# A two-layer hybrid transformer step on one core: low parts to VectorE, bank copies to ScalarE, layer 1's output projection by token groups, values woven into a norm

## The chip, the core and the metric

The kernel runs on one NeuronCore of a Trainium2 chip. Its engines are TensorE (PE: matmuls, which write PSUM banks), VectorE (DVE), ScalarE (ACT), GpSimd (POOL) and SyncE (SP, which issues most of the DMAs). Each engine works through its own queue in order. The metric is the device time of one execution in microseconds; the figure for a kernel is the median of its runs.

## The reference

One inference step for 1024 latent tokens and 128 context tokens, model width 1024, two layers with the same skeleton:

```python
hs = modulate(xs, norm_mix[i], sh1_s, sc1_s)      # RMSNorm, scaled and shifted by the condition
ms = mixer(hs)                                    # layer 0: pooling and latent attention; layer 1: neighbourhood attention
xs = xs + g1_s * ms                               # ms ends in an output projection, 1024 x 1024
xs = xs + g2_s * channel_mixer(modulate(xs, norm_mlp[i], sh2_s, sc2_s), mlp1[i], mlp2[i])
```

Layer 0 has 8 heads of latent attention with normed keys and queries (64 channels and 32 rotary ones); layer 1 has 16 heads whose queries and keys are normed, and each latent token attends to a window of 8 x 16 tokens and to all context tokens. `channel_mixer` is a squared-ReLU MLP of width 4096. Outputs are the two token sets and the new caches, all in float32.

## The kernel before, in words

Tokens lie along the free axis: every activation is a set of tiles of 128 channels by 1152 tokens (1024 latent, 128 context). Matmuls of full precision are made of three: each operand is split into a high part (rounded) and a low part (the rest), and `mm3` (L330 to L337) issues weight high by low, weight low by high, high by high. So a split is a cast (the high part) and a subtraction (the low part): `wsplit` (L156) for weights, `split_store` (L712 on) for key and query tiles of layer 0, `split_groups` (L908 on) and `split_acts` (L932 on) for the inputs of an output projection.

The program writes the work down in Python generators that `weave` (L130) interleaves by given lengths; a tile scheduler then settles the order on each engine from that text, from the dependencies, and from the buffers: PSUM has three pools of banks (`pa` 3, `pb` 3, `pc` 2), weights a ring of 3 raw and 4 + 4 split tiles, everything else 36 slots.

The stages, with the us at which they lie in the profile:

- to 200: modulation, layer 0's input projection and latents.
- 200 to 263, **key and query tiles**: `key_tile` (six tiles) and `query_tile` (six) multiply a tile by its norm factor, which a pair of `ps_b` matmuls (`bcast`, L707 and L708) spreads over the partitions, then `split_store` casts the tile (L715, ACT), subtracts (L716, the engine is an argument), and stores both parts to DRAM; `load_qk` and `load_rest` read them back by head. The keys' subtraction is on POOL, the queries' of tiles 4 and 0 on DVE, and that of tiles 1, 5, 2, 3 on POOL. `value_gen` (`ps_v`, L840 on) is woven with the maxima of the first head (`max_units`, L1073).
- 263 to 560: latent attention, head by head. `finish_values` (L1038 on) takes a finished PSUM bank: the numerators to the output tile (L1040, DVE), the sums to `den` (L1041, ACT); for every second head `recip_pair` (L1079 on) divides.
- 560 to 670 layer 0's output projection, by token groups (`out_group`), to 1430 its MLP. `first` (L446 to L448) and `second` (L476 to L478) are the MLP's two matmuls; `operand_gen` makes the former's operands (L352, ACT, and L353, DVE) from the normed input.
- 1430 to 1720, **layer 1's queries and keys** in four groups `g` (`ps_n1`), each followed by a norm: squares, `head_rstd`, 12 times a `bcast` and its product on DVE (L1266), and the split and store of four tiles (L1270, L1271). Then `value_gen1` (36 units; `ps_v`, L1427 to L1429) is woven with the maxima of heads 0 and 1 (`na_max`, L1320 and L1321).
- 1815 to 2125, **neighbourhood attention**: `na_units` computes scores (L1347, L1348), adds the bias table on DVE (L1373), takes the exponential on ACT (L1400) and multiplies by the values (L1380); `finish_values` as above. `na_max` of later heads runs between; its row of maxima goes through DRAM (`mrow`).
- 2090 to 2203, **layer 1's output projection** (`ps_o`, L335 to L337): `out_first` takes the first four input tiles (k = 0 to 3) for all tokens, 24 PSUM tiles of 384 columns, and adds them to the residual stream `x` (L342); it is woven into the last head and covers its end. `out_second` takes the other four, by chunks of 288 tokens, 32 PSUM tiles (L896); behind chunk 0 and chunk 1 stand the statistics of the MLP's norm (`norm_stats`, one `ps_n` matmul each, L274), and `operand_gen` runs between the tiles of chunks 2 and 3. The last pair of heads, which is finished last, is one of the four inputs of `out_second`.
- 2203 to the end: layer 1's MLP.

Of the kernel before, what the change touches and what calls it, by code (L numbers as in the profile page):

```python
# [32 lines left out]
XS, PSH, OW, OA, OB = (11, 11, 12, 12, 13, 13, 14, 14), (14, 14, 15, 15), 10, 8, 6  # L33
# [57 lines left out]
def hybrid_kernel(ctx: ExitStack, tc: tile.TileContext, I, O):  # L91
# [707 lines left out]
    def query_tile(t, eng):  # L799
        raw = tq[t]  # L800
        for ch in range(NCH):
# [15 lines left out]
          (chain(iter([None] * 7), *[key_tile(t, nc.gpsimd) for t in (4, 0, 1, 5, 2, 3)]), 38))  # L817
# [57 lines left out]

    def out_first(layer, acts):
        for q in range(4):
            ws = wout_chunk(layer, 0, q)
            for mi in range(2):
                for ch in range(NCH):  # L880
                    ps = PS("ps_o")[:, :CH]
                    mm3(ps, ws[mi], acts, ch * CH, ch * CH + CH)
                    residual(x, 2 * q + mi, ch, ps, layer, 0)
                    yield

    def out_second(layer, acts):
# [18 lines left out]
        free_acts(acts)  # L905
        return ops
# [24 lines left out]

    def split_acts(ops):  # L932
        acts = []
        for o in ops:
# [3 lines left out]
            nc.vector.tensor_sub(a[1], o, a[0])
# [99 lines left out]
    def finish_values(par, half, po, opair, den, last, store=None):  # L1038
        qs = slice(half * 512, half * 512 + 512)
        nc.vector.tensor_copy(opair[par:par + 64, qs], po[par:par + 64])  # L1040
        nc.scalar.copy(den[par:par + 64, qs], po[64 - par:128 - par])  # L1041
# [89 lines left out]
    for t in (1, 5, 2, 3):  # L1131
        run(query_tile(t, nc.gpsimd))
# [100 lines left out]
    r8 = S.alloc("r8h", F32R), S.alloc("r8l", F32R)  # L1233
    silu_load()
    for g in range(4):
# [16 lines left out]
        for ch in range(NCH):  # L1252
            cs = slice(ch * CH, ch * CH + CH)
            ps8 = PS("ps8", "pb")[0:8, :CH]
            for t in range(4):
                square_sum(ps8, t, raw[t][:, cs], t == 0, t == 3)
            head_rstd(ps8, 64, cs, nts[(NCH * g + ch) % 2], r8, rows)
        for ch in range(NCH):
            for t in range(4):
                wn = "naq" if t < 2 else "nak"  # L1260
                pp_ = pq if t < 2 else pk
                ps = PS("ps_b", "pb")[:, :CH]
                bcast(ps, t, r8, slice(ch * CH, ch * CH + CH), rows)
                for a, b, i in chunk_parts(ch):
                    o = pp_[:, pairs[t] * P:pairs[t] * P + P] if i else raw[t][:, a:b]
                    nc.vector.scalar_tensor_tensor(o, raw[t][:, a:b], V(wn), ps[:, a - ch * CH:b - ch * CH],  # L1266
                                                   op0=ALU.mult, op1=ALU.mult)
        for t in range(4):
            hi, lo = fhs[t % 2], raw[t].bitcast(F32R)
            nc.scalar.copy(hi[:, :NS], raw[t][:, :NS])  # L1270
            nc.vector.tensor_sub(lo[:, :NS], raw[t][:, :NS], hi[:, :NS])  # L1271
            dst, o = (qd, 0) if t < 2 else (kd, P)
            dma(dst[0][pairs[t], :, o:o + NS], hi[:, :NS])
            dma(dst[1][pairs[t], :, o:o + NS], lo[:, :NS])
# [133 lines left out]


    vt = []  # L1410

    def value_gen1():
        for qt in range(4):
            ws = [wsplit(I["wv1"][qt, i]) for i in range(2)]
            fs = slice(qt * 256, qt * 256 + 256)
            vt.append([S.alloc(f"vt{qt}{i}") for i in range(3)])
            v4 = [t.rearrange("p (a e f) -> p a e f", e=3, f=64) for t in vt[qt]]
            for t in v4:
                nc.gpsimd.memset(t[:, :, 1], 1.0)
            for i in range(2):  # L1420
                dma(v4[2][:, 4 + i, 0:3:2], I["v_cache"][:, qt * 256 + i * P:qt * 256 + i * P + P].rearrange("p (e f) -> p e f", f=64))
            for tt in range(9):
                ck = slice(tt * P, tt * P + P)
                ps = PS("ps_v1")[:, :256]
                for k in range(KD):
                    wh, wl = (w[:, (k % 4) * 256:(k % 4) * 256 + 256] for w in ws[k // 4])
                    nc.tensor.matmul(ps, hh[k][:, ck], wl, start=k == 0, stop=False)  # L1427
                    nc.tensor.matmul(ps, hl[k][:, ck], wh, start=False, stop=False)
                    nc.tensor.matmul(ps, hh[k][:, ck], wh, start=False, stop=k == KD - 1)  # L1429
                if tt == 8:  # L1430
                    nc.scalar.copy(pv[:, fs], ps)
                else:
                    nc.scalar.copy(v4[tt // 3][:, tt % 3 * 2:tt % 3 * 2 + 2, 0:3:2], ps.rearrange("p (g e f) -> p g e f", e=2, f=64))
                yield
# [222 lines left out]
```

## Time and profile before

| | us |
|---|---|
| three runs | 2985.49, 2983.98, 2985.34 |
| median | 2985.34 |
| profiled execution | 2996.6 |
| its span | 2994.7 |
| mean granted TensorE clock | 0.977 of full speed |

A row of the profile names the line of the program, the engine, the operation, the tiles it writes and reads, and their shape; then how many there are, their time together, the mean of one in ns, and the time for which the engine sat idle before them, with what ended it. A wait row has the waiting engine and line, what it waited for, the sum, how often, and the longest. A row of the timeline has the start, the length, and in brackets the idle time ahead of it. A row of the view by stretches has each engine's busy time in the stretch, the clock granted to TensorE, and the DMA engines' mean share. Idle time of an engine that is not the bottleneck costs nothing.

### The profile page before, as it was taken

The page shows a single profiled execution, that of the slowest core. Times are in us where ns is not written, and L with a number is a line of the kernel's source. Part 1 is how long each engine was busy: PE and PEld are TensorE (multiplying, and loading weights), DVE is VectorE, ACT ScalarE, POOL GpSimd, SP SyncE. Part 2 cuts the span into 40 slices and gives each one's busy share as a digit, 9 for nine tenths or more (in the row PEclk, how much of TensorE's full clock was granted, in tenths as well). Part 3 has the DMA queues.
Part 4 walks back from the last instruction along what each step waited for, and adds up shares of the span by engine and source line. Part 5 has one row for each costly group of instructions (what it writes and reads, how often), then busy time and mean ns, then how long its engine had stood idle before and what let it go on. Part 6 is the DMA issues. An engine that isn't in the chain of part 4 may idle for free. (4 is left out here: it accounts for less than half of the span.)

```text
span 2994.7 us, 46426 instructions
## 1 busy us (share of the span) xinstructions
PE 2909.3 (97%) x18302; PEld 2610.2 (87%) x18302; DVE 2151.7 (72%) x3923; ACT 1321.2 (44%) x2136; POOL 329.3 (11%) x238
## 2 busy tenths in 40 slices
PE   7999999999999999999999999998989999999999
PEld 4955666799999999999988897666989999999999
DVE  5977863477778899786898524667587678877775
ACT  5463444345355544354644423444244445453433
POOL 2004010141000020000221000111020000200000
PEclk9997999999999999999999999898989999999999
DMA  6527521222232344233555325775213222332322
GB/s 236 170 86 254 144 76 41 77 77 88 84 105 77 101 141 148 78 99 92 170 204 183 116 101 128 194 187 165 70 36 99 80 91 85 117 101 78 98 78 89
DMA packets 117435, 347.59 MB, mean 116 GB/s; under 512 B 16697, under 2 KB 37801, under 8 KB 117218
## 3 DMA queue, kind: packets, MB, share of 16 engines
q1 hardware_dynamic: 114674, 340.76, 36.9%
q0 software_dynamic: 2544, 3.87, 0.4%
q8 instruction: 144, 2.36, 0.3%
q14 instruction: 73, 0.60, 0.1%
HBM read 296.54 MB, written 46.85 MB: 115 GB/s over the span
## 5 line engine op out<-in xcount | busy, mean ns | idle before, releaser
L477 PE MATMUL ps<-mh,wl 128*128 128x288 f32 x2048 | 599.8, 294 | 0.0
L478 PE MATMUL ps<-mh,wh 128*128 128x288 f32 x2048 | 595.6, 295 | 0.0
L476 PE MATMUL ps<-ml,wh 128*128 128x288 f32 x2048 | 590.4, 295 | 2.6 <-DVE x L482 1.4
L446 PE MATMUL ps<-bl,wh 128*128 128x288 f32 x1792 | 534.4, 299 | 16.1 <-DVE bl L353 5.2
L447 PE MATMUL ps<-bh,wl 128*128 128x288 f32 x1792 | 530.9, 296 | 0.0
L448 PE MATMUL ps<-bh,wh 128*128 128x288 f32 x1792 | 529.2, 295 | 0.0
L477 PEld LDWEIGHTS ps<-mh,wl 128*128 128x128 f32 x2048 | 384.2, 188 | 0.1
L476 PEld LDWEIGHTS ps<-ml,wh 128*128 128x128 f32 x2048 | 380.1, 188 | 3.6 <-DVE x L482 1.4
L478 PEld LDWEIGHTS ps<-mh,wh 128*128 128x128 f32 x2048 | 382.4, 188 | 0.0
L482 DVE SCALAR_TENSOR_TENSOR x<-ps,ada,x 128x288 f32<-128x288 f32 (+2 forms) x640 | 270.8, 451 | 122.7 <-PE ps L478 121.5
L446 PEld LDWEIGHTS ps<-bl,wh 128*128 128x128 f32 x1792 | 337.9, 189 | 20.5 <-issue 9.3
L448 PEld LDWEIGHTS ps<-bh,wh 128*128 128x128 f32 x1792 | 339.7, 190 | 0.0
L447 PEld LDWEIGHTS ps<-bh,wl 128*128 128x128 f32 x1792 | 338.8, 189 | 0.2
L160 ACT CAST wh<-wr 128x1024 fp32r<-128x1024 f32 x188 | 197.1, 1049 | 190.2 <-PE ps L448 77.3
L419 ACT CAST wh<-s 128x512 fp32r<-128x512 f32 x256 | 146.1, 618 | 278.6 <-PE ps L478 194.9
L161 DVE TENSOR_TENSOR wl<-wr,wh 128x1024 fp32r<-128x1024 f32 x144 | 179.2, 1248 | 60.1 <-ACT wh L160 60.1
L200 DVE CUSTOM_DVE_ANT_0 trash<-wada,silu 128x1024 bf16<-128x1024 f32 x160 | 206.1, 1288 | 13.3 <-DMA wada<-in_wada 6.9
L419 ACT CAST wh<-wr 128x1024 fp32r<-128x1024 f32 (+1 forms) x128 | 106.9, 835 | 199.7 <-PE ps L478 135.7
L161 POOL TENSOR_TENSOR wl<-wr,wh 128x1024 fp32r<-128x1024 f32 x44 | 117.2, 2670 | 689.8 <-ACT wh L160 689.8
L420 DVE TENSOR_TENSOR wl<-s,wh 128x512 fp32r<-128x512 f32 x232 | 157.2, 709 | 3.7 <-ACT wh L419 1.5
L1115 PE MATMUL ps_pv<-p,vt 128*128 128x512 f32 x288 | 147.7, 596 | 0.1
L1074 DVE TENSOR_REDUCE stat<-ps_m 128x1 f32<-128x384 f32 x192 | 98.6, 551 | 65.2 <-PE ps_m L1073 64.9
(321 smaller groups left out, 6044.2 us busy)
## 6 DMA issues: line engine op xcount, KB each, us to landing
wr<-in_w SPq DMA_DIRECT2D x256, 512.0 KB, 3.7
wada<-in_wada SPq DMA_DIRECT2D x48, 512.0 KB, 3.5
wada<-in_wada0t SPq DMA_DIRECT2D x32, 512.0 KB, 3.7
wr<-in_win SPq DMA_DIRECT2D x24, 512.0 KB, 4.5
wr<-in_wout SPq DMA_DIRECT2D x24, 512.0 KB, 4.3
kk<-kd SPq DMA_DIRECT2D x32, 288.0 KB, 7.3
wadan<-in_wada SPq DMA_DIRECT2D x16, 512.0 KB, 8.8
ta<-in_bias_q SPq DMA_DIRECT2D x16, 512.0 KB, 4.4
```

Source lines behind the costliest of these rows:

```text
L160: nc.scalar.copy(hi, r)
L161: (nc.gpsimd if e else nc.vector).tensor_sub(lo, r, hi)
L200: nc.vector.tensor_tensor_reduce(trash, r[:, :D], silu[i][:, :D], scale=1.0, scalar=0.0, op0=ALU.mult, op1=ALU.add, accum_out=a)
L419: nc.scalar.copy(h, src)
L420: (nc.gpsimd if j in EDGE and min(ps) in EDGE_POOL else nc.vector).tensor_sub(l, src, h)
L446: nc.tensor.matmul(ps, wh[:, a], hl[:, b], start=k == 0, stop=False)
L447: nc.tensor.matmul(ps, wl[:, a], hh[:, b], start=False, stop=False)
L448: nc.tensor.matmul(ps, wh[:, a], hh[:, b], start=False, stop=k == 3)
L476: nc.tensor.matmul(ps, wh, hl, start=kk == 0, stop=False)
L477: nc.tensor.matmul(ps, wl, hh, start=False, stop=False)
L478: nc.tensor.matmul(ps, wh, hh, start=False, stop=kk == 3)
L482: nc.vector.scalar_tensor_tensor(x[m][:, a:b], ps[:, a - ch * HC:b - ch * HC], g, x[m][:, a:b], op0=ALU.mult, op1=ALU.add)
```

## The change

Four things change.

1. `key_tile` and the second loop of `query_tile` get `nc.vector` instead of `nc.gpsimd`: the subtraction of ten tiles is DVE's.
2. The norm of layer 1 becomes a generator, `norm_group`. For groups 0 to 2 it runs as before; for group 3 it is woven with the first 9 units of `value_gen1`, of which the other 27 follow with the maxima.
3. `finish_values` copies the numerators with ACT too.
4. Layer 1's output projection: `out_first` computes only the chunks 0 and 1 (token group 0) of the first four inputs, 16 PSUM tiles of 288 columns; `out_second` adds the other four inputs of these chunks, with both norm statistics, and then computes chunks 2 and 3 (group 1) from all eight inputs in one PSUM tile each, while `operand_gen` runs between. The weights of group 1 are loaded and split once more. The inputs are split by `split_groups`, and the number of tiles woven into the last head (`OA`) goes from 8 to 10.

```diff
-XS, PSH, OW, OA, OB = (11, 11, 12, 12, 13, 13, 14, 14), (14, 14, 15, 15), 10, 8, 6
+XS, PSH, OW, OA, OB = (11, 11, 12, 12, 13, 13, 14, 14), (14, 14, 15, 15), 10, 10, 6
...
-          (chain(iter([None] * 7), *[key_tile(t, nc.gpsimd) for t in (4, 0, 1, 5, 2, 3)]), 38))
+          (chain(iter([None] * 7), *[key_tile(t, nc.vector) for t in (4, 0, 1, 5, 2, 3)]), 38))
...
+    def out_tile(layer, m, ch, ws, acts, k):
+        ps = PS("ps_o", ("pa", "pc")[m % 2] if k else "pa")[:, :HC]
+        mm3(ps, ws, acts, ch % 2 * HC, ch % 2 * HC + HC)
+        for a, b, i in chunk_parts(ch, HC):
+            nc.vector.scalar_tensor_tensor(x[m][:, a:b], ps[:, a - ch * HC:b - ch * HC], adav(layer, 2, m, i),
+                                           x[m][:, a:b], op0=ALU.mult, op1=ALU.add)
...
     def out_first(layer, acts):
         for q in range(4):
             ws = wout_chunk(layer, 0, q)
             for mi in range(2):
-                for ch in range(NCH):
-                    ps = PS("ps_o")[:, :CH]
-                    mm3(ps, ws[mi], acts, ch * CH, ch * CH + CH)
-                    residual(x, 2 * q + mi, ch, ps, layer, 0)
+                for ch in range(2):
+                    out_tile(layer, 2 * q + mi, ch, ws[mi], acts, 0)
                     yield
...
     def out_second(layer, acts):
         ws = [wout_chunk(layer, 1, q) for q in range(4)]
-        st, right, ops, og = {}, [], {}, None
-        for ch in range(4):
+        st = {}
+        for ch in range(2):
             for m in range(KD):
-                if ch == 3 or ch == 2 and m in (3, 6):
-                    next(og, None)
...
-            if ch < 2:
-                st[ch] = norm_stats(x, ch, HC)
-            if ch == 1:
-                og = operand_gen(ops, quad_apply(x, 0, layer, st[0]), right)
-            elif ch == 2:
-                right.extend(quad_apply(x, 1, layer, st[1]))
+                out_tile(layer, m, ch, ws[m // 2][m % 2], [a[0] for a in acts[4:]], 1)
+            st[ch] = norm_stats(x, ch, HC)
+        for a in acts[4:]:
+            S.free_ap(a[0][0])
+        ops = {}
+        og = operand_gen(ops, quad_apply(x, 0, layer, st[0]), quad_apply(x, 1, layer, st[1]))
+        n = 0
+        for q in range(4):
+            ws = [wout_chunk(layer, half, q) for half in range(2)]
+            for mi in range(2):
+                for ch in (2, 3):
+                    out_tile(layer, 2 * q + mi, ch, [w for half in range(2) for w in ws[half][mi]], [a[1] for a in acts], 1)
+                    n += 1
+                    if n % 2 == 0:
+                        next(og, None)
         run(og)
...
     def finish_values(par, half, po, opair, den, last, store=None):
         qs = slice(half * 512, half * 512 + 512)
-        nc.vector.tensor_copy(opair[par:par + 64, qs], po[par:par + 64])
+        nc.scalar.copy(opair[par:par + 64, qs], po[par:par + 64])
         nc.scalar.copy(den[par:par + 64, qs], po[64 - par:128 - par])
...
     for t in (1, 5, 2, 3):
-        run(query_tile(t, nc.gpsimd))
+        run(query_tile(t, nc.vector))
...
+        norm = norm_group(g, raw, rows, pairs)
+        if g < 3:
+            run(norm)
+        else:
+            vg = value_gen1()
+            weave((norm, 10), (islice(vg, 9), 9))
...
-    weave((value_gen1(), 36), (chain(na_max(0, tls[0]), na_max(1, tls[1])), 10))
+    weave((vg, 27), (chain(na_max(0, tls[0]), na_max(1, tls[1])), 10))
...
-            acts = split_acts(pairs)
-            of = out_first(1, acts)
+            acts = [split_groups(o) for o in pairs]
+            of = out_first(1, [a[0] for a in acts])
...
-    acts = split_acts(pairs + opairs[7:])
+    acts += [split_groups(o) for o in pairs + opairs[7:]]
     ops = out_second(1, acts)
```

What this does to the order on the engines is shown at three places. First DVE, among the first key tiles, as a difference (`kro` and `tk` are key tiles, `fh` their high part, `tq` query tiles):

```order
 L771 SCALAR_TENSOR_TENSOR sw<-ps_q,vec,rs_1413 128x384 x2
 L792 SCALAR_TENSOR_TENSOR tk_192_1458<-small_1416,vec,ps_b 128x128
+L716 TENSOR_TENSOR kro_1676<-kro_1676,fh_1718 128x1152
+L785 SCALAR_TENSOR_TENSOR tk_193_1459<-tk_193_1459,vec,ps_b 128x384
 L772 TENSOR_TENSOR tq_204_1629<-tq_204_1629,sw 128x384
-L785 SCALAR_TENSOR_TENSOR tk_193_1459<-tk_193_1459,vec,ps_b 128x384
 L767 SCALAR_TENSOR_TENSOR tq_205_1630<-tq_205_1630,vec,rc_1412 128x384
 L252 TENSOR_SCALAR nt_1462<-ps_1773 8x384
+L716 TENSOR_TENSOR tk_192_1458<-tk_192_1458,fh_1768 128x1152
 L772 TENSOR_TENSOR tq_204_1629<-tq_204_1629,sw 128x384
```

The subtractions L716 now stand in DVE's queue, between the products of the next tiles.

Second PE, at the norm of layer 1's group 3. Before, the last broadcasts (`ps_b`) and the maxima of head 0 (`ps_m`) behind them:

```order
L1428 MATMUL ps_v_16828<-wh,hl_956_13882 128x256
L1429 MATMUL ps_v_16828<-wh,hh_948_13874 128x256
L707 MATMUL ps_b<-r8h_14389,bcs_14365 128x384
L708 MATMUL ps_b<-r8l_14390,bcs_14365 128x384
...
L707 MATMUL ps_b<-r8h_14389,bcs_14365 128x384 x3
L708 MATMUL ps_b<-r8l_14390,bcs_14365 128x384 x3
...
L1320 MATMUL ps_m<-kk_16653,qq_16654 128x256
L1321 MATMUL ps_m<-kk_16653,qq_16654 128x256
```

and the same place now (the value matmuls are at L1278 to L1280):

```order
L707 MATMUL ps_b<-r8h_14389,bcs_14365 128x384 x2
L1280 MATMUL ps_v_16864<-wh,hh_941_13867 128x256
L1278 MATMUL ps_v_16864<-wl,hh_942_13868 128x256
L1279 MATMUL ps_v_16864<-wh,hl_950_13876 128x256
L1280 MATMUL ps_v_16864<-wh,hh_942_13868 128x256
L708 MATMUL ps_b<-r8l_14390,bcs_14365 128x384 x2
L1278 MATMUL ps_v_16864<-wl,hh_943_13869 128x256
L1279 MATMUL ps_v_16864<-wh,hl_951_13877 128x256
L1280 MATMUL ps_v_16864<-wh,hh_943_13869 128x256
L707 MATMUL ps_b<-r8h_14389,bcs_14365 128x384
L708 MATMUL ps_b<-r8l_14390,bcs_14365 128x384
```

Sixteen broadcast matmuls stood in a row before; now 4 to 20 value matmuls lie between one pair and the next.

Third PE, from the last value matmul of the attention to the first MLP product: the counts of output matmuls `ps_o` between the marks are 307, 142, and 106 (before; the marks are the two `ps_n` matmuls, and among the last 106 lie the first seven MLP matmuls), and 188, 141, and 297 (now, the MLP behind them). The place where the last pair of heads is first needed, before (`ol_20320` is its low part) and now (`oa_20213`):

```order
L337 MATMUL ps_o<-oh_19848,wh 128x384
L335 MATMUL ps_o<-ol_20320,wh 128x288
L335 MATMUL ps_o<-ol_19837,wh 128x384
L336 MATMUL ps_o<-oh_19836,wl 128x384
L337 MATMUL ps_o<-oh_19836,wh 128x384
```

```order
L335 MATMUL ps_o<-oa_20207,wh 128x288
L336 MATMUL ps_o<-oa_20207,wl 128x288
L337 MATMUL ps_o<-oa_20207,wh 128x288
L335 MATMUL ps_o<-oa_20213,wh 128x288
L336 MATMUL ps_o<-oa_20213,wl 128x288
L337 MATMUL ps_o<-oa_20213,wh 128x288
```

Behind the last value matmul that is the 133rd output matmul before, and the 96th now.

More of the change, by code (lines that the diff above doesn't have):

```diff
@@ L1233, in hybrid_kernel, with norm_group @@
     r8 = S.alloc("r8h", F32R), S.alloc("r8l", F32R)
+    def norm_group(g, raw, rows, pairs):
+        for ch in range(NCH):
+            cs = slice(ch * CH, ch * CH + CH)
+            ps8 = PS("ps8", "pb")[0:8, :CH]
+            for t in range(4):
+                square_sum(ps8, t, raw[t][:, cs], t == 0, t == 3)
+            head_rstd(ps8, 64, cs, nts[(NCH * g + ch) % 2], r8, rows)
+            yield
+        for ch in range(NCH):
+            for t in range(4):
+                wn = "naq" if t < 2 else "nak"
+                pp_ = pq if t < 2 else pk
+                ps = PS("ps_b", "pb")[:, :CH]
+                bcast(ps, t, r8, slice(ch * CH, ch * CH + CH), rows)
+                for a, b, i in chunk_parts(ch):
+                    o = pp_[:, pairs[t] * P:pairs[t] * P + P] if i else raw[t][:, a:b]
+                    nc.vector.scalar_tensor_tensor(o, raw[t][:, a:b], V(wn), ps[:, a - ch * CH:b - ch * CH],
+                                                   op0=ALU.mult, op1=ALU.mult)
+            yield
+        for t in range(4):
+            hi, lo = fhs[t % 2], raw[t].bitcast(F32R)
+            nc.scalar.copy(hi[:, :NS], raw[t][:, :NS])
+            nc.vector.tensor_sub(lo[:, :NS], raw[t][:, :NS], hi[:, :NS])
+            dst, o = (qd, 0) if t < 2 else (kd, P)
+            dma(dst[0][pairs[t], :, o:o + NS], hi[:, :NS])
+            dma(dst[1][pairs[t], :, o:o + NS], lo[:, :NS])
+            yield
@@ new lines, in hybrid_kernel, with value_gen1 @@
+    vt = []
+    def value_gen1():
+        for qt in range(4):
+            ws = [wsplit(I["wv1"][qt, i]) for i in range(2)]
+            fs = slice(qt * 256, qt * 256 + 256)
+            vt.append([S.alloc(f"vt{qt}{i}") for i in range(3)])
+            v4 = [t.rearrange("p (a e f) -> p a e f", e=3, f=64) for t in vt[qt]]
+            for t in v4:
+                nc.gpsimd.memset(t[:, :, 1], 1.0)
+            for i in range(2):
+                dma(v4[2][:, 4 + i, 0:3:2], I["v_cache"][:, qt * 256 + i * P:qt * 256 + i * P + P].rearrange("p (e f) -> p e f", f=64))
+            for tt in range(9):
+                ck = slice(tt * P, tt * P + P)
+                ps = PS("ps_v1")[:, :256]
+                for k in range(KD):
+                    wh, wl = (w[:, (k % 4) * 256:(k % 4) * 256 + 256] for w in ws[k // 4])
+                    nc.tensor.matmul(ps, hh[k][:, ck], wl, start=k == 0, stop=False)
+                    nc.tensor.matmul(ps, hl[k][:, ck], wh, start=False, stop=False)
+                    nc.tensor.matmul(ps, hh[k][:, ck], wh, start=False, stop=k == KD - 1)
+                if tt == 8:
+                    nc.scalar.copy(pv[:, fs], ps)
+                else:
+                    nc.scalar.copy(v4[tt // 3][:, tt % 3 * 2:tt % 3 * 2 + 2, 0:3:2], ps.rearrange("p (g e f) -> p g e f", e=2, f=64))
+                yield
@@ L1251, in hybrid_kernel @@
             background(QBG)
[L1252 to L1274, printed above, removed]
+        norm = norm_group(g, raw, rows, pairs)
+        if g < 3:
+            run(norm)
+        else:
+            vg = value_gen1()
+            weave((norm, 10), (islice(vg, 9), 9))
         if g == 2:
@@ L1406, in na_units @@
             yield
[L1410 to L1434, printed above, removed]
     tls = {0: load_na(0), 1: load_na(1)}
-    weave((value_gen1(), 36), (chain(na_max(0, tls[0]), na_max(1, tls[1])), 10))
+    weave((vg, 27), (chain(na_max(0, tls[0]), na_max(1, tls[1])), 10))
     S.free(*hh, *hl)
@@ L1512, in hybrid_kernel @@
     run(of)
-    free_acts(acts)
-    acts = split_acts(pairs + opairs[7:])
+    for a in acts:
+        S.free_ap(a[0][0])
+    acts += [split_groups(o) for o in pairs + opairs[7:]]
     ops = out_second(1, acts)
```

20 lines of the change are left out of this document (2 added, 18 removed).

## Prediction

> **What bounds the kernel now.** I read the page first, then the busy time and granted clock by stretch, then the waits inside the stretches that stand out. The page:
>
> ```profile
> span 2994.7 us, 46426 instructions
> PE 2909.3 (97%) x18302; PEld 2610.2 (87%) x18302; DVE 2151.7 (72%) x3923; ACT 1321.2 (44%) x2136; POOL 329.3 (11%) x238
> PEclk9997999999999999999999999898989999999999
> ```
>
> TensorE (PE) is busy 97% of the span, so the matmuls are the floor, and what an edit of the other engines can win is PE's idle time plus the time at a lower granted clock. Both are concentrated in a few stretches, which the view by stretch shows (columns: stretch; length, busy us and instruction count of each engine; granted clock; DMA share; GB/s):
>
> ```profile
> core 0: us, PE busy (x) PEld busy (x) DVE busy (x) ACT busy (x) POOL busy (x), PEclk, DMA share, GB/s
> 225.00:250.00 25.00, 21.08 (x69) 11.90 (x67) 22.06 (x35) 10.59 (x15) 16.84 (x12) 0.79 0.75 266
> 250.00:275.00 25.00, 22.92 (x61) 15.19 (x62) 18.09 (x39) 9.79 (x21) 12.51 (x7) 0.70 1.03 380
> 275.00:300.00 25.00, 23.71 (x74) 15.81 (x74) 15.27 (x34) 6.46 (x18) 1.75 (x3) 0.75 0.45 114
> 1719.00:1723.00 4.00, 1.48 (x6) 0.98 (x5) 3.71 (x8) 0.93 (x2) 0.05 (x1) 0.75 0.00 0
> 1723.00:1731.00 8.00, 7.71 (x31) 6.58 (x30) 7.00 (x15) 4.57 (x7) 1.51 (x4) 0.50 0.58 232
> 1825.00:2100.00 275.00, 250.86 (x1013) 167.74 (x1013) 186.38 (x476) 113.58 (x209) 35.99 (x43) 0.91 0.71 184
> 2200.00:2225.00 25.00, 18.31 (x104) 17.40 (x104) 22.66 (x27) 10.97 (x16) 12.50 (x6) 0.75 0.20 63
> 2225.00:2250.00 25.00, 22.24 (x153) 22.01 (x153) 18.06 (x26) 14.52 (x20) 6.61 (x5) 0.91 0.20 64
> 2250.00:2275.00 25.00, 25.00 (x190) 25.00 (x190) 19.43 (x31) 10.22 (x12) 3.91 (x2) 1.00 0.33 106
> 650.00:675.00 25.00, 23.85 (x178) 23.41 (x177) 18.91 (x27) 7.91 (x12) 13.23 (x7) 1.00 0.19 64
> 675.00:700.00 25.00, 24.95 (x186) 24.51 (x185) 20.09 (x30) 16.86 (x23) 8.74 (x6) 1.00 0.29 87
> ```
>
> Four places lose time: layer 0's key and query tiles (225 to 300), group 3's norm in layer 1 (1719 to 1731), the neighbourhood attention (1825 to 2100), and the start of layer 1's MLP (2200 to 2250). A short wait costs twice: in 1719 to 1723 PE is idle for 2.5 us, and in the 8 us behind it the clock is 0.50, which loses another 4. The change touches all four. I go by them in order of time, as gains in us of the profiled execution, 2996.6 us (1.9 around its span); it lies 11.3 above the median of the runs, 2985.34, and I subtract the sum from both.
>
> **Key and query tiles.** The low parts (L716) of all six key tiles and of the last four query tiles go from GpSimd (POOL) to VectorE (DVE):
>
> ```profile
> L716 POOL TENSOR_TENSOR tk<-tk,fh x4: 2649/2652/2752, 213.8 to 244.9; 128x1152 fp32r<-128x1152 f32 x4
> L716 POOL TENSOR_TENSOR tq<-tq,fh x4: 2376/2382/2393, 254.8 to 262.7; 128x1024 fp32r<-128x1024 f32 x4
> L716 DVE TENSOR_TENSOR tq<-tq,fh x2: 1218/1218/1218, 248.6 to 250.3; 128x1024 fp32r<-128x1024 f32 x2
> L767 DVE SCALAR_TENSOR_TENSOR tq<-tq,vec,rc x6: 599/1486/4755, 188.8 to 234.0; 128x384 f32<-128x384 f32 x6
> L767 DVE SCALAR_TENSOR_TENSOR tq<-tq,vec,rc 128x384 f32<-128x384 f32 x6 | 11.4, 1896 | 4.6 <-ACT tq L765 4.6
> ```
>
> The DVE form takes 1.22 us for 1024 columns, so 1.37 for 1152: DVE gains 6 x 1.37 + 4 x 1.22 = 13.1 us. Against it stands the slowing that goes away: an L767 takes 0.60 us alone and up to 4.76 beside a POOL subtraction; the six sum to 11.4, 7.8 more than 6 x 0.60. DVE's net load thus grows by some 5 us in 200 to 263, where it is busy 22 of 25. What shrinks is the chain of each tile, by 1.2 to 1.4 us, and the value matmuls of this place are scheduled between the query tiles instead of behind them. In 225 to 300 the clock alone loses 0.21 x 25 + 0.30 x 25 + 0.25 x 25 = 19 us and idle time is 7.3; but a DMA share of 1.03 in 250 to 275 says that the stores and reloads of these tiles are at their own limit, which a faster subtraction does not move. So I take 4 of these 26: bounds +9 (all idle time, and 2 of the clock's) and -5 (DVE's net load lands on the path).
>
> **Group 3's norm, values woven.** The 16 broadcast matmuls of group 3 stood back to back, and each pair needs two PSUM results taken off by DVE:
>
> ```profile
> PE ps_b L707 <- DVE r8h L703: 2.5, 1, 2.5
> 1719.47 0.33 PE L708 MATMUL ps_b<-r8l,bcs 8*128 8x384 f32 x1
> 1722.32 1.33 PE L707 MATMUL ps_b<-r8h,bcs 8*128 8x384 f32 x3 [2.51 <-DVE r8h L703]
> ```
>
> Now value matmuls lie between them, 4 to 20 at a time; the work is the same, merely taken from the 27 units behind. The wait (2.5) and the half clock behind it (half of the 8 us in 1723 to 1731, and about 1 us on either side) go: 2.5 + 4 + 1.5 = 8. Bounds 3 (the wait alone) and 10 (the 0.3 us pauses behind it too). What hides the norm then is the woven matmuls; if DVE is later than they last, part of the wait stays, hence the 3.
>
> [...]
>
> **Copies of the finished banks.** `finish_values` copies two halves of each bank, one by DVE (L1040) and one by ScalarE (L1041); now ScalarE does both:
>
> ```profile
> L1040 DVE COPY no<-ps_pv x32: 671/688/697, 1838.1 to 2124.7; 64x512 f32<-64x512 f32 x32
> L1041 ACT COPY den<-ps_pv x48: 577/582/588, 307.3 to 2125.4; 64x512 f32<-64x512 f32 x48
> ACT den L1041 <- DVE no L1040: 31.6, 21, 3.8
> DVE no L1040 <- PE ps_pv L1380: 13.2, 12, 3.5
> ACT p L1400 <- DVE p L1373: 66.2, 39, 5.6
> PE ps_st L1348 <- DMA q<-mrow: 9.1, 6, 2.9
> PE ps_m L1320 <- DMA qq<-qd: 4.3, 3, 1.6
> PE ps_st L1347 <- DVE p L1373: 3.2, 2, 2.6
> PE ps_m L1320 <- DVE stat L1323: 3.0, 3, 1.5
> ```
>
> In layer 0 (16 copies) I count nothing: PE paces that attention, and the page's clock row is at 9 over it. In layer 1, DVE loses 32 x 0.69 = 22 us of work and 13 of standing for PE's result, and ACT gains 32 x 0.58 = 19 but stops waiting 31.6 for DVE; ACT is busy 114 of 275, so there is room. ACT's exponentials (L1400) wait for DVE's additions (L1373), so a freer DVE feeds them earlier, unless a copy stands in front of them in ACT's queue. PE's own waits for DVE here are 3.2 + 3.0; 13.4 are for DMA and stay. I take 3, half of the 6.2. Bounds +12 (the 6.2, and as much again of the clock, since 24 us of idle go with 0.09 x 275 = 25 of clock) and -6 (five more waits of the size of an ACT copy pair, 1.16, with the clock's loss left out).
>
> **Layer 1's output projection by token groups.** Matmuls: before, 288 of 384 columns and 384 of 288; now 768 of 288. The start times of two of the wide ones that lie 15 matmuls apart give their pitch:
>
> ```profile
> 2137.79 0.33 PE L336 MATMUL ps_o<-oh,wl 128*128 128x384 f32 x1
> 2140.39 0.33 PE L336 MATMUL ps_o<-oh,wl 128*128 128x384 f32 x1
> ```
>
> 2.60 / 15 = 0.173; the narrow ones take 25 / 190 = 0.132 by the row of 2250 to 2275. 288 x 0.173 + 384 x 0.132 = 100.5 before, 768 x 0.132 = 101.4 now, 1 worse. Eight more weight chunks are loaded and split (SP, ACT, DVE); DVE saves 16 residual instructions of about the same sum, and PE paces this stage at clock 1.00, so I count nothing for them.
>
> The gain is at the start of the MLP. 2200 to 2250 holds 104 + 153 matmuls, which at the 190 per 25 us of the next stretch need 33.8 us: 16.2 are lost. The cause is the operands, which the norm of the second chunk must feed:
>
> ```profile
> 2191.37 0.65 PE L274 MATMUL ps_n<-nt,ones 128*128 128x288 f32 x2
> PE ps L446 <- DVE bl L353: 5.2, 1, 5.2
> 2211.20 3.19 DVE L353 TENSOR_TENSOR bl<-t,bh 128x1152 fp32r<-128x1152 f32 x1
> ```
>
> Before, 106 output matmuls (14.0 us) follow the norm matmul of the second chunk. Now all of group 1 does: 297, 39.2 us. The chain from that norm (its matmul at 2191.4) to the end of this L353 (2214.4) is 23 us with everything that DVE does between, and the other operands follow within some 12 more: covered. Layer 0 already runs so (`out_group`), and its 650 to 700 loses 50 - 364 / 7.6 = 2.1. So 16.2 - 2.1 = 14, less 1: 13, bounds 7 and 15.
>
> **The last pair's cover.** Behind the last value matmul PE had 132 matmuls of 384 columns, 22.9 us, before it needs the last pair of heads; now only 50 of the first half and 45 of the second's k = 4 to 6, 95 x 0.132 = 12.5. The chain that makes the pair:
>
> ```profile
> 2124.66 0.69 DVE L1040 COPY no<-ps_pv 64x512 f32<-64x512 f32 x1 [1.89 <-PE ps_pv L1380]
> 2128.31 2.39 POOL L1084 TENSOR_TENSOR den<-den,ry 128x1024 f32<-128x1024 f32 x1 [37.47 <-ACT ry L1083]
> 2136.38 1.35 DVE L938 TENSOR_TENSOR ol<-no,oh 128x1152 fp32r<-128x1152 f32 x1
> ```
>
> From 2124.66 to 2137.73, 13.1 us, with residuals and a weight split in DVE's queue between. It becomes slightly shorter (the first copy off DVE) and its splits are halves. The wait is thus 0 to 3 us, and 5 more if the clock halves as at 1722: I take -2.5, bounds 0 and -8.
>
> **Sum.** 4 + 8 + 3 + 13 - 2.5 = 25.5: 2996.6 becomes 2971.1, and the median 2985.3 becomes **2960**.
>
> **The rivals.**
>
> *Half given back.* The tiles stay bound by their stores (0 instead of 4), and ACT's copies delay exponentials (-6 instead of +3): 25.5 - 13 = 12.5, time 2973. For it: the DMA share of 1.03, and ACT's queue in order. Against it: ACT waits 66 us for DVE there. 0.18.
>
> *The clock does not follow these waits.* If the low clock only happened to stand behind them, just the idle goes: 3 at the norm; at the MLP the idle of 2200 to 2250 alone, 6.7 + 2.8 = 9.5, less 1 and less layer 0's idle of 1.2; 1.5 lost at the last pair; 2 for the tiles and 3 for the copies. That is 3 + 7.3 - 1.5 + 5 = 14, time 2971. The 0.50 behind 1722 speaks against it. 0.07. [...]
>
> *The attention leaves the low clock.* With DVE 35 us freer, the 6.2 us of waits go and the clock of 1825 to 2100 rises from 0.91 to 0.95, 11 us: 17 instead of 3, sum 39.5, time 2946. Against it: 13.4 us of the waits there are for DMA. 0.12.
>
> *Slower: ACT becomes the path of the neighbourhood attention.* A bank's second copy stands ahead of the next exponentials, 32 x 0.58 = 19 us; if all of that reaches PE, the clock loses as much again (24 of idle went with 25 of clock): 37. The sum without this part is 22.5, so the kernel comes out 14.5 slower, 3000. It decides from where 22.5 of the 37 land, and shows from 28. Against it: ACT is idle 161 of 275. 0.05.
>
> *Nothing to see*: the gains are as small as their lower bounds, -5 + 3 - 6 + 7 - 2.5 = -3.5 with the last pair's wait as taken, time 2989. 0.03.
>
> **How the numbers follow.** Forecast 0.55, the five rivals 0.18, 0.07, 0.12, 0.05, 0.03. Range 2943 to 2976: from the rival with the better clock and 3 us less, to half given back and 3 us more; outside are the slower ones and the extremes of the bounds. 0.2%, about what a measurement of this kernel can tell from no change, is 6 us. Faster takes the forecast, the clock cases and most of half given back: 0.89; same 0.06, of which 0.03 is from that; slower 0.05.
>
> **What would show it.** Right: no wait of ps_b for r8h and a clock near 1.00 in the value stretch; first MLP product straight behind the output matmuls; a wait of ps_o for the last `oa` of at most 3 us behind the last value matmul; the tile stretch still at a clock below 0.9 with loads landing late. Wrong: exponentials waiting for L1041's neighbour copy in ACT's queue, or a DVE that is full in 200 to 263 and delays the stores.

## The result and the profile after

| | before | changed |
|---|---|---|
| median of the runs, us | 2985.41 | 2957.78 |
| lowest to highest | 2983.98 to 2993.57 | 2956.27 to 2960.67 |
| ratio | | 0.9895, 95% interval 0.9878 to 0.9912 |
| span of the profiled execution | 2994.7 | 2954.5 |

27.6 us faster; 2960 was forecast. The terms behind the sum did not hold as well as the sum, and the rest of this text is about them. The page of the changed kernel:

```profile
span 2954.5 us, 46671 instructions
PE 2887.5 (98%) x18398; PEld 2593.8 (88%) x18398; DVE 2133.0 (72%) x3893; ACT 1354.0 (46%) x2192; POOL 303.3 (10%) x228
PEclk9996999999999999999999999999999999999999
```

TensorE's share went from 97 to 98% and the eights in the clock row of layer 1 are gone; where the key and query tiles are, a 6 stands instead of a 7. The view by stretches of the changed kernel, at the four places of the prediction:

```profile
225.00:250.00 25.00, 21.77 (x65) 11.79 (x63) 22.50 (x38) 11.51 (x18) 8.08 (x9) 0.69 0.81 282
250.00:275.00 25.00, 22.40 (x60) 14.05 (x61) 21.93 (x42) 9.20 (x18) 2.38 (x1) 0.64 1.01 366
275.00:300.00 25.00, 24.13 (x78) 16.93 (x76) 15.00 (x32) 6.79 (x18) 1.24 (x2) 0.71 0.32 80
1716.00:1732.00 16.00, 16.00 (x103) 12.93 (x102) 10.17 (x20) 7.42 (x12) 1.20 (x3) 1.00 0.20 79
1825.00:2100.00 275.00, 257.00 (x1151) 178.72 (x1151) 182.52 (x476) 134.91 (x242) 35.52 (x42) 0.96 0.70 187
2175.00:2200.00 25.00, 24.94 (x188) 24.73 (x187) 17.24 (x24) 10.62 (x16) 12.22 (x8) 1.00 0.22 64
2200.00:2225.00 25.00, 25.00 (x188) 24.78 (x188) 20.15 (x33) 16.24 (x20) 4.83 (x2) 1.00 0.40 127
```

The tiles' stretch is no better (clocks 0.69, 0.64, 0.71, against 0.79, 0.70, 0.75), the norm of group 3 runs at 1.00 with TensorE always busy, the neighbourhood attention is at 0.96 instead of 0.91, and the MLP starts without a gap.

A difference of two stretches is only as good as the two executions. So here is the length of four stages in every profile of this study, taken from matmul start times: **A** from the last `ps_k` (layer 0's key matmuls, ahead of the tiles) to the last value matmul of layer 0 (key and query tiles and latent attention), **B** from the first to the last `ps_v` of layer 1, **C** from there to the last value matmul of the neighbourhood attention, **D** from the last `ps_o` to the start of the last matmul. The last two columns are the granted clock and DVE's busy us in C. The names are those of the experiments below.

| kernel | A | B | C | D | clock in C | DVE in C |
|---|---|---|---|---|---|---|
| before | 381.6 | 127.2 | 303.0 | 783.9 | 0.91 | 204 |
| before_again | 381.8 | 127.6 | 297.4 | 784.7 | 0.91 | 205 |
| a_only | 382.1 | 127.1 | 295.7 | 779.3 | 0.93 | 204 |
| b_only | 382.1 | 122.7 | 302.5 | 782.1 | 0.92 | 204 |
| c_only | 382.1 | 127.5 | 284.2 | 778.8 | 0.95 | 185 |
| d_only | 381.9 | 126.9 | 290.7 | 769.3 | 0.95 | 207 |
| changed | 383.0 | 122.8 | 282.6 | 769.1 | 0.95 | 187 |
| after_again | 383.2 | 122.7 | 296.1 | 769.2 | 0.92 | 188 |
| no_a | 382.8 | 122.8 | 281.9 | 769.6 | 0.95 | 186 |
| no_c | 383.3 | 122.7 | 299.1 | 769.2 | 0.93 | 206 |
| d_late | 384.0 | 122.8 | 291.2 | 780.1 | 0.92 | 189 |
| act_load | 382.7 | 122.7 | 282.3 | 769.1 | 0.96 | 185 |
| c_load | 382.5 | 127.6 | 288.9 | 779.4 | 0.93 | 206 |
| c_dve | 385.1 | 127.2 | 320.9 | 782.2 | 0.89 | 226 |

A is the same within 2.4 in all but one, B has two values, D is 769 with the statistics early and 779 to 785 without, and C scatters: by 6 between two profiles of the same unchanged kernel, by 13 between two of the changed one (`changed` and after_again), which run the same matmuls in the same order. In these two pairs C holds most of the difference of the spans, 8.0 and 14.1. Verdicts on C need medians of many runs.

### The profile page after: what moved, and what is told of

The parts are those of the page before. It is cut to its first block, busy times and chain, and to the rows that moved or that the text cites. A ratio compares the mean times of both kernels' runs of the same rounds, so it can differ in the third digit from the quotient of the medians.

```text
span 2954.5 us, 46671 instructions
## 1 busy us (share of the span) xinstructions
PE 2887.5 (98%) x18398; PEld 2593.8 (88%) x18398; DVE 2133.0 (72%) x3893; ACT 1354.0 (46%) x2192; POOL 303.3 (10%) x228
## 5 line engine op out<-in xcount | busy, mean ns | idle before, releaser
L446 PE MATMUL ps<-bl,wh 128*128 128x288 f32 x1792 | 531.4, 297 | 6.8 <-DVE u L459 4.1
L446 PEld LDWEIGHTS ps<-bl,wh 128*128 128x128 f32 x1792 | 335.6, 187 | 10.1 <-issue 5.0
L160 ACT CAST wh<-wr 128x1024 fp32r<-128x1024 f32 x196 | 205.3, 1049 | 174.1 <-PE ps L448 75.9
L161 DVE TENSOR_TENSOR wl<-wr,wh 128x1024 fp32r<-128x1024 f32 x152 | 188.9, 1245 | 47.7 <-ACT wh L160 47.6
L335 PE MATMUL ps_o<-oa,wh 128*128 128x288 f32 x512 | 152.6, 299 | 2.5 <-DVE oa L925 1.9
L336 PE MATMUL ps_o<-oa,wl 128*128 128x288 f32 x512 | 151.9, 297 | 0.0
```

The source lines that it names most:

```text
L160: nc.scalar.copy(hi, r)
L161: (nc.gpsimd if e else nc.vector).tensor_sub(lo, r, hi)
L335: nc.tensor.matmul(ps, wh, hl[:, c0:c1], start=k == 0, stop=False)
L446: nc.tensor.matmul(ps, wh[:, a], hl[:, b], start=k == 0, stop=False)
```

## The experiments

Ratios are to runs of the kernel before on the same chip, with 95% intervals; 0.001 is 3 us.

**One part alone.** Four kernels, each the kernel before with one part of the diff: a_only the two lines with `nc.vector` for the tiles; b_only `norm_group` and the two `weave` lines; c_only the copy in `finish_values`; d_only `out_tile`, `out_first`, `out_second`, the splits and `OA`. Of the first three, the core:

```diff
-          (chain(iter([None] * 7), *[key_tile(t, nc.gpsimd) for t in (4, 0, 1, 5, 2, 3)]), 38))
+          (chain(iter([None] * 7), *[key_tile(t, nc.vector) for t in (4, 0, 1, 5, 2, 3)]), 38))
...
-        run(query_tile(t, nc.gpsimd))
+        run(query_tile(t, nc.vector))
```

```diff
+            vg = value_gen1()
+            weave((norm, 10), (islice(vg, 9), 9))
...
-    weave((value_gen1(), 36), (chain(na_max(0, tls[0]), na_max(1, tls[1])), 10))
+    weave((vg, 27), (chain(na_max(0, tls[0]), na_max(1, tls[1])), 10))
```

```diff
-        nc.vector.tensor_copy(opair[par:par + 64, qs], po[par:par + 64])
+        nc.scalar.copy(opair[par:par + 64, qs], po[par:par + 64])
```

> The kernel before with only the ten L716 subtractions moved to VectorE. The prediction's theory (each tile's chain is 1.2 to 1.4 us shorter, VectorE is no longer slowed beside GpSimd): 4 us faster, 2981. Rival, read from the two profiled executions, where the first 560 us are 0.5 us longer in the changed kernel although it started 0.9 earlier (VectorE's net load lands on the path): between no change and 2 us slower, 2985 to 2987.

> The kernel before with only group 3's norm woven with the first nine value units. The prediction's theory (the 2.5 us wait and the half clock behind it both go): 8 us faster, 2977. Rival, from the profiles, where the stretch from the first value matmul to the last is 4.4 us shorter in the changed kernel: 4 to 5 us faster, 2981. If the low clock were not tied to the wait: 3 us, 2982.

> The kernel before with only the numerators' copies moved to ScalarE. The prediction's theory (half of the 6.2 us that TensorE waits for VectorE in the neighbourhood attention): 3 us faster, 2982. Rival, from the profiles, where that attention is some 19 us shorter in the changed kernel (of which up to 11 may be that the profiled execution of before was that much above its median): 8 to 19 us faster, 2966 to 2977, with the clock granted in the attention up from 0.91 to 0.95 or more.

> The kernel before with only layer 1's output projection by token groups. The prediction's theory (14 won at the start of the MLP, 1 lost to narrower matmuls, 2.5 lost to a wait for the last pair of heads): 10.5 us faster, 2975, with a wait of TensorE for the last pair's operands of 1 to 3 us. Rival, from the profile of the changed kernel, which shows no such wait: 13 us faster, 2972. If the last pair's chain is longer here, with the first copy still on VectorE, the wait would be up to 3 us and show in this run alone.

| kernel | median, us (before 2988.45) | ratio | interval |
|---|---|---|---|
| a_only | 2982.42 | 0.9979 | 0.9965 to 0.9993 |
| b_only | 2983.54 | 0.9987 | 0.9974 to 1.0001 |
| c_only | 2971.43 | 0.9952 | 0.9936 to 0.9969 |
| d_only | 2974.20 | 0.9953 | 0.9938 to 0.9968 |

So 6, 4, 14 and 14 us, where the prediction had 4, 8, 3 and 10.5; b_only's interval just includes no change. The four sum to 1.29%, more than the change brings (1.05%, and 0.81% in the repeat below).

a_only is the odd one: by the runs 6 faster, but not in its own stage. Its view by stretches:

```profile
225.00:250.00 25.00, 22.00 (x65) 12.04 (x65) 22.44 (x38) 11.36 (x18) 8.08 (x9) 0.70 0.82 279
250.00:275.00 25.00, 22.12 (x60) 13.74 (x60) 21.92 (x41) 9.37 (x19) 2.37 (x1) 0.64 1.00 367
```

DVE is now busy 22 of 25 in the second of these too (18 before), the clock is lower than before, and stage A is as long as ever.

**The kernel before again**, and what VectorE's time is worth in the neighbourhood attention. c_load and c_dve are the kernel before with:

```diff
-        nc.vector.tensor_copy(opair[par:par + 64, qs], po[par:par + 64])
+        nc.scalar.copy(opair[par:par + 64, qs], po[par:par + 64])
         nc.scalar.copy(den[par:par + 64, qs], po[64 - par:128 - par])
+        if adds:
+            spare = cst.tile([P, 4], F32, tag="spare", name="spare")
+            after(nc.vector.reduce_max(spare[par:par + 64], ones[par:par + 64].unsqueeze(1).to_broadcast([64, 4, P]), axis=AX.X), adds[-1])
```

(`adds` holds the bias additions of L1373, so that the reduction stays in its place in DVE's queue) and

```diff
-        nc.scalar.copy(den[par:par + 64, qs], po[64 - par:128 - par])
+        nc.vector.tensor_copy(den[par:par + 64, qs], po[64 - par:128 - par])
```

and no_a is the changed kernel with the two lines of part a undone.

> The kernel before, unchanged, for a second profile. If the spread of its executions (2980 to 2997) comes from the neighbourhood attention, the first 560 us and the MLPs agree with the first profile within 1 us, and the attention differs from the 303 us between the last value projection matmul and the last value matmul there, by about as much as the span does. If it is spread over the stages, no stage differs by more than 3 us.

> Numerators copied by ScalarE as in c_only, and for each copy in the neighbourhood attention VectorE reduces a constant block of 64 x 512 instead (left over, its result is not used): VectorE has about the work of before, but nothing of it waits for a finished bank, and ScalarE waits for nothing of it. If VectorE's load is what cost, the gain of c_only goes: 2982 to 2988. If it was the standing, of VectorE's queue behind the bank and of ScalarE behind VectorE's copy, the gain stays: 2971 to 2975.

> The kernel before with both copies of a finished bank on VectorE. If VectorE's load is what cost, 22 us more of it in the neighbourhood attention make the kernel some 14 slower, 3000. If it was ScalarE's waiting for VectorE's copy (31.6 us there), that wait is gone too, and the kernel is as fast as before or up to 10 faster, 2976 to 2986. If it was VectorE's queue standing behind the finished bank, 3 to 10 slower, since it stands no longer than before but works 0.69 more behind each.

> The changed kernel with the ten L716 subtractions back on GpSimd. The prediction's term for them: 4 slower than the changed kernel, 2962. By the profiles, which show the first 560 us no shorter in any kernel with that part: no change, 2958 (ratio to before 0.9895). By the single run of that part, which came out 6 faster than before: 2964.

| kernel | median, us (before 2985.63) | ratio | interval |
|---|---|---|---|
| before_again | 2988.62 (one run) | | |
| c_load | 2981.42 | 0.9989 | 0.9975 to 1.0003 |
| c_dve | 3014.64 | 1.0101 | 1.0081 to 1.0122 |
| no_a | 2959.03 | 0.9908 | 0.9890 to 0.9925 |

before_again agrees with the first profile in A, B and D within 0.8 and is 5.6 shorter in C, where its span is 8.0 shorter. The rest lies ahead of A and between A and B, some 2 us in each, more than the 1 us that was expected there.

c_load gives back 11 of the 14 us of c_only, and their intervals do not meet: VectorE's load is what cost. The 3 us left may be the waiting, but they are not clear of no change. The reductions, and stage C of before_again, c_only, c_load and c_dve in the view by stretches:

```profile
L1046 DVE TENSOR_REDUCE spare<-ones x32: 664/676/683, 1831.6 to 2102.2; 64x4 f32<-64x512 f32 x32
```

```profile
1818.00:2115.40 297.40, 276.40 (x1143) 190.47 (x1142) 205.16 (x506) 120.16 (x222) 36.50 (x44) 0.91 0.67 181
```

```profile
1818.80:2103.00 284.20, 262.71 (x1139) 183.45 (x1138) 184.54 (x475) 136.53 (x253) 36.41 (x44) 0.95 0.72 189
```

```profile
1818.00:2107.00 289.00, 268.82 (x1141) 187.01 (x1139) 205.85 (x507) 136.93 (x253) 36.26 (x44) 0.93 0.69 186
```

```profile
1823.30:2144.20 320.90, 280.94 (x1143) 193.01 (x1141) 225.92 (x537) 101.91 (x191) 36.89 (x44) 0.89 0.63 168
```

Read the DVE column (the third busy time) against length and clock: in these four, 185, 206, 226 us of DVE go with 284, 289 to 297, 321 us and with clocks of 0.95, 0.91 to 0.93, 0.89. ScalarE's column goes the other way. The table of all profiles is less tidy: with 185 to 189 us of DVE, C is 282 to 296 long at clocks of 0.92 to 0.96, and with 204 to 207 us it is 289 to 303 at 0.91 to 0.95. The two profiles of the changed kernel differ as much, with the same work (first, then after_again):

```profile
1814.50:2097.10 282.60, 263.07 (x1167) 182.25 (x1166) 186.89 (x489) 137.66 (x254) 36.55 (x44) 0.95 0.72 192
```

```profile
1815.20:2111.30 296.10, 269.79 (x1168) 187.26 (x1167) 187.51 (x489) 137.74 (x254) 36.38 (x44) 0.92 0.69 183
```

So the price of DVE's load comes from the runs: 11 us for the 21.6 that c_load adds, half a us for each, although DVE is busy only two thirds of the stage. (The profile of c_load, an execution of 2975, is from the fast end of that kernel's runs.) c_dve is 29 slower where a load price of 14 was expected. Some of it is the 16 copies of layer 0 (A is 3 longer), the recorded wait of TensorE for maxima that come back from DRAM is 15.9 there, against 9.1 before, and the rest is open, since its second copy also waits for the bank.

no_a is as fast as the changed kernel (0.9908 against 0.9895 and, below, 0.9919): part a brings nothing that can be measured beside the others.

**The changed kernel again, and three of its parts in turn.** no_c is the changed kernel with the copy back on DVE. d_late has

```diff
-            st[ch] = norm_stats(x, ch, HC)
+            if ch == 0:
+                st[ch] = norm_stats(x, ch, HC)
...
-        og = operand_gen(ops, quad_apply(x, 0, layer, st[0]), quad_apply(x, 1, layer, st[1]))
+        right = []
+        og = operand_gen(ops, quad_apply(x, 0, layer, st[0]), right)
...
-                    if n % 2 == 0:
+                    if n in (4, 8):
                         next(og, None)
+                    if n == 11:
+                        right.extend(quad_apply(x, 1, layer, norm_stats(x, 1, HC)))
```

and act_load has, in `finish_values`, behind the two copies (`exps` holds the exponentials):

```diff
+        if exps:
+            spare = cst.tile([P, 256], mybir.dt.bfloat16, tag="spare", name="spare")
+            for _ in range(2):
+                after(nc.scalar.copy(spare[par:par + 64].rearrange("p (a b) -> p a b", a=2),
+                                     ones[par:par + 64].unsqueeze(1).to_broadcast([64, 2, P])), exps[-1])
```

The expectation of act_load speaks of 48 pairs; there are 32, in the neighbourhood attention alone.

> The changed kernel, unchanged, beside the next three on one chip. If the parts add up by their single runs (0.21, 0.13, 0.48 and 0.47% of the time before), its ratio to before is 0.987; by its first measurement 0.9895. Without the first part, whose stage shows no gain in any profile, the other three give 0.989.

> The changed kernel with the numerators' copies back on VectorE. The prediction's term: 3 slower than the changed kernel. By the single runs, in which the copies gave 14 and 22 us of other VectorE work took back 11 of them: 11 to 14 slower, 2969 to 2972, with the clock in the neighbourhood attention back at 0.91 to 0.93.

> The changed kernel with the norm statistics of the second chunk moved behind 11 of the 16 output tiles of token group 1, so that 120 output matmuls follow its norm matmul instead of 297. If the cover of the operands is what gave the gain at the MLP's start, as predicted, the wait comes back there: 9 to 16 slower, 2967 to 2974, with TensorE waiting for VectorE's operands at its start and a clock of 0.5 behind. If it was something else in the new order (the weight buffers free earlier, for one): no change, 2958.

> The changed kernel with 48 pairs of small ScalarE copies of a constant block (64 x 256 each, left unused) where the bank copies are made in the neighbourhood attention, in effect another copy per bank. If ScalarE's queue were on the path there, as the prediction's rival on the slow side had it: 10 to 37 slower, 2968 or more. If ScalarE has room (135 of 275 us busy): within 3 us of the changed kernel.

| kernel | median, us (before 2987.05) | ratio | interval |
|---|---|---|---|
| after_again | 2962.53 | 0.9919 | 0.9898 to 0.9940 |
| no_c | 2970.42 | 0.9945 | 0.9926 to 0.9964 |
| d_late | 2973.15 | 0.9956 | 0.9940 to 0.9973 |
| act_load | 2958.20 | 0.9907 | 0.9884 to 0.9929 |

The repeat is 0.24% from the first measurement, and their intervals overlap. no_c is 8 slower than the changed kernel beside it, with intervals that overlap, and 15 by the first measurement's ratio; c_only alone had 14. So the copies are worth 8 to 15 in the changed kernel. no_c's clock in C is 0.93, as expected, but after_again's is no better, 0.92.

act_load adds 64 ScalarE copies, 25.7 us, and costs nothing that can be measured; the copies, and its stage C:

```profile
L1043 ACT CAST spare<-ones x64: 387/401/406, 1830.1 to 2093.6; 64x256 bf16<-64x256 f32 x64
1813.40:2095.70 282.30, 262.26 (x1167) 181.40 (x1166) 185.43 (x489) 160.35 (x318) 36.34 (x44) 0.96 0.71 192
```

ScalarE is busy 160 of 282 us there, DVE as in the changed kernel, and length and clock are those of its first profile. ScalarE's queue is not on the path.

d_late brings the gap at the MLP's start back. Its view by stretches, TensorE's waits, and the copy that ended the longest of them:

```profile
2175.00:2200.00 25.00, 20.61 (x150) 20.38 (x149) 23.31 (x28) 13.02 (x21) 13.18 (x6) 0.97 0.12 43
2200.00:2225.00 25.00, 20.44 (x144) 19.39 (x143) 22.66 (x30) 13.16 (x20) 7.26 (x4) 0.96 0.20 64
...
PE ps L446 <- ACT scr L451: 4.4, 1, 4.4
PE ps L446 <- DVE u L458: 2.1, 1, 2.1
PE ps L446 <- DVE bl L353: 1.9, 2, 1.4
...
2197.45 0.40 ACT L451 COPY scr<-ps 128x288 f32<-128x288 f32 x1 [1.45 <-DVE bl L353]
```

150 + 144 matmuls in 50 us, at 7.6 a us, lose 11.3 us, and D is 11 longer, by that delay of the statistics and the operands behind them alone; weights and buffers are as in the changed kernel. The longest wait carries ScalarE's name, but its copy (L451) had itself waited for DVE's subtraction of an operand (L353). The cover of the operands is the cause. The half clock behind the wait is shorter than was expected: 9 of the 11.3 us are idle time.

## Why the prediction was right, and where its terms were not

**Key and query tiles: 4 predicted, 0 found.** The step that failed is "I take 4 of these 26". Stage A is 381.6 to 385.1 in every kernel, with the part and without it. The slowing beside GpSimd did go: the six L767 now take 0.60 to 0.62 us each (up to 4.76 before), as forecast.

```profile
L767 DVE SCALAR_TENSOR_TENSOR tq<-tq,vec,rc x6: 601/611/619, 187.9 to 236.4; 128x384 f32<-128x384 f32 x6
```

Two things that the prediction named can have taken the gain back, and no run separates them. One is DVE's net load, its lower bound and one of its signs of being wrong: in 225 to 275 DVE went from 40 to 44 busy us of 50. The other is the stores and reloads, the first half of the rival *half given back*: the DMA share stayed at 1.01 in 250 to 275. The 6 us by which a_only beat before are not in that stage. Its order on TensorE differs from before also in the neighbourhood attention, and C scatters by more than that; whether they are more than C's scatter was not settled. In the changed kernel, leaving the part out costs nothing (0.9908 against 0.9895 and 0.9919).

**The woven norm: 8 predicted, 4.5 found** (B: 127.2 to 122.8; by the runs 3.9, 0 to 8). The mechanism held: no wait, clock 1.00. The size was off in "the half clock behind it (half of the 8 us ... and about 1 us on either side)". The 32 matmuls from 1722.3 to 1731.2 took 8.9 us, 0.3 of it waits; at the pitches of the changed kernel's rows they take 5.3. So some 3.3 were lost, not 5.5. And the weave has a price that I had put at nothing. Start times before, within the row of broadcasts:

```profile
1718.16 0.33 PE L708 MATMUL ps_b<-r8l,bcs 8*128 8x384 f32 x1
1718.33 0.33 PE L707 MATMUL ps_b<-r8h,bcs 8*128 8x384 f32 x1
1718.51 0.33 PE L708 MATMUL ps_b<-r8l,bcs 8*128 8x384 f32 x1
```

and of a pair between value matmuls in the changed kernel:

```profile
1721.33 0.28 PE L1278 MATMUL ps_v<-wl,hh 128*128 128x256 f32 x1
1721.54 0.44 PE L707 MATMUL ps_b<-r8h,bcs 8*128 8x384 f32 x1
1721.83 0.33 PE L708 MATMUL ps_b<-r8l,bcs 8*128 8x384 f32 x1
1722.09 0.39 PE L1279 MATMUL ps_v<-wh,hl 128*128 128x256 f32 x1
1722.31 0.28 PE L1280 MATMUL ps_v<-wh,hh 128*128 128x256 f32 x1
```

In a row a broadcast starts 0.17 behind the last. In a pair among value matmuls the two take 0.29 and 0.26, and the value matmul ahead and the one behind take 0.21 and 0.22 instead of 0.12: about 0.4 a pair. Some of the pairs were among value matmuls before, so I estimate that 1 to 2 us of the 6.1 (2.5 + 0.3 + 3.3) go back, which leaves what stage B shows.

**The copies: 3 predicted, 8 to 15 found.** This is the step that failed most: "PE's own waits for DVE here are 3.2 + 3.0 ... I take 3, half of the 6.2". It prices an engine by the waits in which its name stands. In the changed kernel those waits are down to 2.8, and the gain is larger than all of them. The rival of the better clock, at 0.12, had 17 us with the clock at 0.95; it was nearer than the forecast, but the clock is only part of the gain and not a steady one. Before, stage C loses 0.09 x 303 = 27 us to the clock and is idle for 26.5. The changed kernel's first profile has 0.05 x 283 = 14 and 19.5, its second 0.08 x 296 = 24 and 26.3. An estimate over more profiles: six kernels or repeats have the numerators on DVE (before twice, a_only, b_only, d_only, no_c) and six on ScalarE (c_only, the changed kernel twice, no_a, d_late, act_load). Their means of C are 298 and 286, of the loss to the clock 22 and 17, of idle time 26 and 22. These kernels differ in other parts too. The waits of TensorE in the neighbourhood attention after:

```profile
PE ps_st L1384 <- DMA q<-mrow: 10.1, 5, 5.6
PE ps_st L1383 <- DVE p L1409: 2.4, 2, 1.8
PE ps_m L1356 <- DVE stat L1359: 0.4, 1, 0.4
```

c_load against c_only shows by the runs that DVE's load costs time in this stage, 11 us for 21.6 more, although DVE is busy for only 185 of 284 us without them and 206 of 289 with them. How a us of DVE becomes low clock or idle time, wait by wait, was not shown. The slow rival, ScalarE on the path, is out: act_load adds 25.7 us to ScalarE and nothing to the time.

**The output projection: 13 predicted, 10.5 with the next point, and 14 found for both together** (the runs of d_only, by their interval 10 to 19). D is 9.2 to 15.6 shorter with the part than without it. The first MLP product stands right behind the last output matmul, as forecast:

```profile
2181.25 0.30 PE L337 MATMUL ps_o<-oa,wh 128*128 128x288 f32 x1
2181.39 0.29 PE L446 MATMUL ps<-bl,wh 128*128 128x288 f32 x1
```

**The last pair: 2.5 lost predicted, 0 found in the changed kernel and 1.2 in d_only.** The chain in the changed kernel, from its first copy (ACT) to its last subtractions (DVE, two in one row), and, of d_only, TensorE's wait for them:

```profile
2097.54 0.58 ACT L1036 COPY no<-ps_pv 64x512 f32<-64x512 f32 x1 [3.88 <-PE ps_pv L1416]
...
2109.11 1.42 DVE L925 TENSOR_TENSOR oa<-no,oa 128x576 fp32r<-128x576 f32 x2
```

```profile
PE ps_o L335 <- DVE oa L925: 1.2, 2, 0.8
```

The first of the two subtractions ends at 2109.8, 12.3 after the copy began; the cover was worked out as 12.5. In the changed kernel there is no such wait; in d_only, with the first copy still on DVE, there is 1.2. It is just covered.

So the sum of 25.5 was right by luck: 7.5 too much on the first two parts cancelled against about as much too little on the other three. (Those were to bring 13.5; 27.6 and 24.5 were measured in all, and less the 4.5 of the weave that leaves 20 to 23.) The mechanism held for the weave and for the output projection, and not for the tiles and the copies.

## What to carry to other kernels

An engine that is busy two thirds of a stage can still cost time there (here DVE, 185 of 284 us, to which 21.6 us more cost 11): test it by adding work to it, not by adding up the waits that carry its name. Price a stage's granted clock together with its waits, and take more than one profile: here the clock of one and the same kernel came out at 0.95 and at 0.92 in the same stage. And before weaving one stream of small matmuls into another, read the pitch at the seams: the switch has a price of its own, here about 0.4 us a pair.

## What the runs showed of the hardware

The same wait does not always cost the same clock. At the MLP's start TensorE waits 5.2 us in the kernel before and 4.4 in d_late; before_again is idle for 6.2 us of 2197 to 2210, as before is of 2206 to 2219, and c_only for 5.2 of 2182 to 2195. The stretches there, in before (its wait and what follows, then the low clock alone); in before_again; in c_only, the last row again the low clock alone; and around the wait in d_late:

```profile
2206.00:2219.00 13.00, 6.79 (x38) 6.24 (x38) 12.64 (x13) 4.10 (x5) 6.50 (x4) 0.75 0.27 81
2212.50:2226.20 13.70, 10.20 (x39) 9.53 (x40) 11.36 (x12) 3.40 (x5) 0.68 (x1) 0.50 0.17 48
```

```profile
2197.00:2205.00 8.00, 3.43 (x26) 3.19 (x24) 8.00 (x8) 2.67 (x3) 6.62 (x4) 0.87 0.22 67
2205.00:2210.00 5.00, 3.37 (x13) 3.06 (x13) 4.64 (x6) 1.55 (x2) 0.00 (x0) 0.50 0.33 105
2210.00:2220.00 10.00, 8.92 (x53) 8.34 (x54) 7.19 (x8) 4.20 (x7) 3.77 (x3) 0.84 0.01 2
```

```profile
2182.00:2190.00 8.00, 6.64 (x50) 6.40 (x48) 8.00 (x14) 5.30 (x7) 7.32 (x5) 1.00 0.20 66
2190.00:2195.00 5.00, 1.13 (x5) 1.16 (x6) 5.00 (x5) 0.00 (x0) 2.51 (x1) 0.84 0.58 172
2193.40:2196.90 3.50, 3.03 (x12) 2.90 (x12) 3.14 (x5) 1.15 (x1) 0.00 (x0) 0.51 0.44 150
```

```profile
2192.00:2197.00 5.00, 1.52 (x12) 1.28 (x10) 5.00 (x6) 2.10 (x2) 3.92 (x3) 1.00 0.14 42
2197.00:2205.00 8.00, 5.17 (x25) 4.59 (x26) 8.00 (x8) 3.10 (x5) 3.51 (x2) 0.79 0.34 106
```

That is 13.7 us at a clock of 0.50 in before, 2 of them inside the wait; 3.5 at 0.51 in c_only; and less than 4 in d_late, if 0.79 over 8 us is part 1.00 and part 0.50. By the same estimate before_again has 10.3: 2.1 from the 0.87 of 2197 to 2205, the 5 us at 0.50, and 3.2 from the 0.84 of 2210 to 2220.

Nor does a shorter wait always cost less. In before, group 3's norm has a wait of 2.5 us, and a wait of 2.8 ends at 2233.5 (an L446 waits for DVE's L458). The low clock at the first and at the second:

```profile
1721.00:1731.30 10.30, 8.70 (x32) 7.56 (x33) 8.92 (x19) 4.87 (x7) 1.55 (x4) 0.50 0.48 191
```

```profile
2233.00:2236.40 3.40, 2.87 (x12) 2.87 (x13) 2.04 (x5) 1.17 (x1) 0.00 (x0) 0.50 0.55 154
```

10.3 us at the shorter, 3.4 at the longer; before_again, with the same wait of 2.5 at the norm, has 0.50 over the 8 us from 1720 to 1728. What sets the length was not shown.
